# Splitting weights into two rounded parts: the low part made by a negating copy on ACT and an adding DMA, instead of a subtraction on DVE

## The chip, the cores and the metric

The kernel runs on one core of a Trainium2 chip. The metric is the device time of one execution in microseconds; a run reports the median of several. The profile is one execution taken by the hardware profiler. Its span runs from the first to the last instruction. The engines are TensorE (PE, with its weight loads as PEld), VectorE (DVE), ScalarE (ACT), GpSimd (POOL) and SyncE (SP). SP and POOL issue the DMAs here; each engine works through its own instructions in order.

## The reference

A decoder layer on 512 tokens of 1024 features, all in float32:

```
h = h + 1/2 * SwiGLU(RMSNorm(h))
u = RMSNorm(h); P = u @ W_in      # [b | c | v], [z | xBC | dt], [g_a | g_b]
y_a = W_out_a( b * conv3(c * v) )
y_b = W_out_ssm( GroupRMSNorm( SSD(conv4(xBC)) * silu(z) ) )
h = h + W_mix_out( sigmoid(g_a) * y_a + sigmoid(g_b) * y_b )
h = h + CrossAttn(RMSNorm(h), RMSNorm(mem))      # 4 heads, 256 memory tokens
h = h + 1/2 * SwiGLU(RMSNorm(h))
out = RMSNorm(h)
```

SSD is the chunked state-space product: chunks of 128 tokens, 32 heads in 4 groups, a state that is carried from chunk to chunk, and decays exp(acs[l] - acs[s]) inside a chunk. What matters here are the matrix products with weights, some 145 MB of them: each weight is read from DRAM once and used once.

## The kernel before

Activations lie feature-major, as tiles of 128 features by 512 tokens. Weights are the stationary operand of TensorE. TensorE multiplies in a rounded form of float32 (fp32r), so every product of 256 or more columns is made of three: hi*hi, hi*lo and lo*hi, where hi is an operand rounded to fp32r and lo is what the rounding took off.

Weights come in tiles of 128 partitions by up to 1024 columns (512 KB), which are 8 blocks of 128 by 128. `load_w` makes one such tile. It loads the raw tile `wr` by a DMA on SP's queue (L95), casts it to `wh` on ACT (L84), and subtracts `wl = wr - wh` on DVE (L85). Each of the three has three buffers. `job` then runs 24 products over the tile, three for each block: wh with the high part of the activations (L110), wh with their low part (L111), wl with their high part (L112). A job's result stands in one of five PSUM banks `pj`. The same `split` helper (L83 to L85) also splits activations, so L84 and L85 occur with other tiles too (sh and sl, ynh and ynl).

The stages, in order: a feed-forward part (44 column tiles of w_gu, then 8 of w_d, each of three weight tiles); the projections and the state-space part; the short convolution and the mixing (with h brought back from DRAM by nine DMAs on POOL's queue, L441 and L445); keys and values (w_k and w_v, with only 256 columns per product, or weights as the moving operand); queries, attention and its output; the second feed-forward part; and a final norm.

In the state-space part each group makes decay tiles `m`: SP loads a row of `acd` broadcast to all partitions (L360), POOL subtracts (L362), ACT takes two functions (L365, L366), DVE multiplies (L367), and TensorE uses them (L379). Between these, TensorE transposes x (L317), DVE makes xdt and xe from it (L320, L325), and a state product follows (L329). `btok` is a copy on ACT of transposed B (L309). The `w_os` jobs behind each group have half tiles of 256 KB.

The program's order on each engine is not that of the source. A scheduler interleaves the instructions when the program is built, by its own estimate of when each operand is ready, so work of the next group's projections stands between the steps of a group.

The first weight tile is loaded in two halves, ahead of everything else but one tile of h.

Of the kernel before, what the change touches and what calls it, by code (L numbers as in the profile page):

```python
"""Hybrid decoder layer (macaron SwiGLU, short-conv + SSD mixer, memory cross-attention, macaron
SwiGLU, final RMSNorm) on one core.

Activations lie feature-major ([128 features, 512 tokens] tiles), weights are the stationary operand.
Every float32 product of 256 or more moving columns is three float32r passes over operands split
exactly in two: hi*hi + hi*lo + lo*hi; narrower products are plain float32.
"""
# [1 line left out]

# [9 lines left out]
AF = mybir.ActivationFunctionType  # L19
ALU = mybir.AluOpType  # L20
# [3 lines left out]
T = 512  # L24
# [4 lines left out]
M = 256  # L29
NH = 32  # L30
NG = 4
MB = 4  # decay tiles in flight
PJ = 5  # PSUM banks of the projections; the other banks serve the rest
NC = 4
EPS = 1e-6

# [11 lines left out]
def layer(ctx: ExitStack, tc: tile.TileContext, a, out):  # L48
# [38 lines left out]
    def load_w(src, n, parts=1):  # L87
        if ahead:
            return ahead.pop(0)
        raw = wp.tile([P, 1024], F32, tag="wr", name=nm("wr"), bufs=3)  # L90
        hi = wp.tile([P, 1024], F32R, tag="wh", name=nm("wh"), bufs=3)
        lo = wp.tile([P, 1024], F32R, tag="wl", name=nm("wl"), bufs=3)
        for i in range(parts):
            c = slice(i * n // parts, (i + 1) * n // parts)
            nc.sync.dma_start(out=raw[:, c], in_=src[:, c])  # L95
            split(raw[:, c], hi[:, c], lo[:, c])
        return hi, lo

    def job(pt, w, xs, m=P):
        """pt += sum over k of w[k]^T xs[k]; w: DRAM [128, nk * m]; xs: (hi, lo) per k."""  # L100
        nk = len(xs)
        pieces = -(-nk // 8)
        per = -(-nk // pieces)
        for k0 in range(0, nk, per):
            k1 = min(nk, k0 + per)
            hi, lo = load_w(w[:, k0 * m:k1 * m], (k1 - k0) * m)
            for k in range(k0, k1):
                s_ = slice((k - k0) * m, (k - k0 + 1) * m)
                xh, xl = xs[k]
                TE.matmul(pt, hi[:, s_], xh, start=(k == 0), stop=False)  # L110
                TE.matmul(pt, hi[:, s_], xl, start=False, stop=False)  # L111
                TE.matmul(pt, lo[:, s_], xh, start=False, stop=(k == nk - 1))  # L112

    def gained(src, gname, k, pool, tag="u", bufs=8, n=T):
        """split src * gain into (hi, lo)"""
        hi = pool.tile([P, n], F32R, tag=tag + "h", name=nm("uh"), bufs=bufs)
        lo = pool.tile([P, n], F32R, tag=tag + "l", name=nm("ul"), bufs=bufs)
        g = pc(gname, k)
        S.activation(out=hi, in_=src, func=AF.Copy, scale=g)
        V.scalar_tensor_tensor(out=lo, in0=src, scalar=g, in1=hi, op0=ALU.mult, op1=ALU.subtract)  # L120
        return hi, lo

    def rms(tiles, n, pool, n_tok=T):
        """1 / sqrt(mean of squares + eps) over the features of tiles, for every token, on all
        partitions: [128, n_tok]"""
        nt = n_tok // P
        acc = None
        for k, t in enumerate(tiles):
            sq = pool.tile([P, T], F32, tag="sq", name=nm("sq"), bufs=3)[:, :n_tok]
            S.activation(out=sq, in_=t, func=AF.Square)  # L130
            if acc is None:
                acc = sq
            else:
                V.tensor_tensor(out=sq, in0=acc, in1=sq, op=ALU.add)  # L134
                acc = sq
        p1 = ps("ss")
        for c in range(nt):
            TE.matmul(p1[:, c:c + 1], acc[:, c * P:(c + 1) * P], ones[:, 0:1], start=True, stop=True)
        sd = pool.tile([P, 4], F32, tag="sd", name=nm("sd"), bufs=2)[:, :nt]
        S.activation(out=sd, in_=p1[:, :nt], func=AF.Sqrt, scale=1.0 / n, bias=eps)  # L140
        rc = pool.tile([P, 4], F32, tag="rc", name=nm("rc"), bufs=2)[:, :nt]
        V.reciprocal(out=rc, in_=sd)
        rb = pool.tile([P, T], F32, tag="sq", name=nm("rb"), bufs=3)[:, :n_tok]
        V.tensor_copy(out=rb.rearrange("p (c t) -> p c t", c=nt),
                      in_=rc.unsqueeze(2).to_broadcast([P, nt, P]))
        p2 = ps("ss")
        for c in range(nt):
            TE.transpose(p2[:, c * P:(c + 1) * P], rb[:, c * P:(c + 1) * P], ident)
        r = pool.tile([P, T], F32, tag="r", name=nm("r"), bufs=2)[:, :n_tok]
        S.copy(out=r, in_=p2[:, :n_tok])  # L150
        return r
# [44 lines left out]

    ffn("ffn1_norm", a["w_gu1"], a["w_d1"])

    # ---------------------------------------------------------------- mixer
    mo = ctx.enter_context(ExitStack())  # L200
    mop = mo.enter_context(tc.tile_pool(name="mo", bufs=1, reuse_waits="tile"))
    yb = [mop.tile([P, T], F32, tag=f"yb{k}", name=f"yb{k}") for k in range(KD)]
# [11 lines left out]
        return p  # L214

    def conv(wname, j0, ntap, acc, x):
        """acc[:, t] = sum over j of w[j] x[t - (ntap - 1) + j]; x in SBUF"""
        S.activation(out=acc, in_=x, func=AF.Copy, scale=pc(wname, j0 + ntap - 1))  # L218
        for j in range(ntap - 2, -1, -1):
            d = ntap - 1 - j  # L220
            V.scalar_tensor_tensor(out=acc[:, d:], in0=x[:, :T - d], scalar=pc(wname, j0 + j),  # L221
                                   in1=acc[:, d:], op0=ALU.mult, op1=ALU.add)

    with tc.tile_pool(name="mx", bufs=1, reuse_waits="tile") as mx:
# [1 line left out]
        def mt(tag, bufs, shape=(P, T), dt=F32):  # L226
            return mx.tile(list(shape), dt, tag=tag, name=nm(tag), bufs=bufs)

        # dt, decays
        pdt = ps()  # L230
        job(pdt[0:NH, :], a["w_dt"], u, m=NH)
        dtT = mt("cv", 2)
# [40 lines left out]
        acs3, dt3, dte3, eend3 = hc(acs), hc(dt), hc(dte), hc(eend)  # L273

        def xbc(ci, tag, bufs):
            """conv4 + silu of xBC feature tile ci"""
            p = proj(40 + ci)
            x = mt("cx", 2)
            V.tensor_tensor(out=x, in0=p, in1=r, op=ALU.mult)
# [12 lines left out]

        def ssd_state(g, bt, ct, xs):
            hs = slice(8 * g, 8 * g + 8)
            # C B^T, transposed, causal: [s, (c, l)]
            pcb = ps("ss")
            for c in range(NC):
                cs = slice(c * P, (c + 1) * P)
# [9 lines left out]
            btok = mt("btok", 1)  # L308
            S.copy(out=btok[:, :3 * P], in_=pbt[:, :3 * P])  # L309

            # token-major x * dt, x * dt * decay to the end of the chunk, states
            xdt, prev = [], []
            for c in range(NC):
                cs = slice(c * P, (c + 1) * P)
# [119 lines left out]
    with tc.tile_pool(name="mb", bufs=1, reuse_waits="tile") as mb:  # L434
# [9 lines left out]
        mem = xm.tile([P, KD, M], F32, tag="mem", name="mem")  # L444
        G.dma_start(out=mem, in_=a["memT"].rearrange("(k p) t -> p k t", p=P))  # L445

        # b * conv3(c * v)
        r2 = wt("r2", 1)
        S.activation(out=r2, in_=r, func=AF.Square)
        ya = []  # L450
# [35 lines left out]
            V.tensor_tensor(out=h[k], in0=p, in1=h[k], op=ALU.add)  # L486
    mo.close()

    # ---------------------------------------------------------------- cross attention
    with tc.tile_pool(name="xa", bufs=1, reuse_waits="tile") as xa:  # L490
        kT, vm = [], []
        with tc.tile_pool(name="xn", bufs=1, reuse_waits="tile") as xm:
# [123 lines left out]
                job(p, a["w_o"][k], o)  # L616
                V.tensor_tensor(out=h[k], in0=p, in1=h[k], op=ALU.add)

    # the final norm is applied token-major: 1 / rms is a scalar of the partition there
    ot = [None]  # L620
    acc = [None]

# [64 lines left out]


def _chunks(w, m=P):
    """(K, N) -> (N / m, 128, K / 128 * m): chunk c, row p holds w[k * 128 + p, c * m:(c + 1) * m]"""  # L690
    k, n = w.shape
    return np.ascontiguousarray(
        w.reshape(k // P, P, n // m, m).transpose(2, 1, 0, 3)).reshape(n // m, P, k // P * m)


def _rows(v):
    """(n * 128,) -> (128, n)"""
    return v.reshape(-1, P).T


def _taps(w):
    """(taps, n * 128) -> (128, n * taps)"""
    k, n = w.shape
    return w.reshape(k, n // P, P).transpose(2, 1, 0).reshape(P, -1)

# [42 lines left out]
```

## Time and profile before

| | us |
|---|---|
| median of 3 runs | 1629.68 (1629.1 to 1631.24) |
| span of the profiled execution | 1625.7 |
| TensorE busy | 1594.7 |
| DVE busy | 855.8 |
| ACT busy | 660.4 |
| POOL busy | 51.6 |

For the profiled execution itself only the span is given; the median of the timed runs lies 4.0 us above it. The granted clock of TensorE is 0.995 of full speed over the span.

A row of a group reads: line, engine, operation, output and inputs by their names in the program, shapes, count; then busy time and the mean of one; then the engine's idle time just before them and what ended most of it. A row of a DMA gives the size of one and the median time from its issue to its landing. A row of the timeline gives the start, the duration, and in brackets the idle time before and what ended it. A row of the waits gives who waited for whom, then the total, the times and the longest.

### The profile page before, as it was taken

The page shows a single profiled execution, that of the slowest core. Times are in us where ns is not written, and L with a number is a line of the kernel's source. Part 1 is how long each engine was busy: PE and PEld are TensorE (multiplying, and loading weights), DVE is VectorE, ACT ScalarE, POOL GpSimd, SP SyncE. Part 2 cuts the span into 40 slices and gives each one's busy share as a digit, 9 for nine tenths or more (in the row PEclk, how much of TensorE's full clock was granted, in tenths as well). Part 3 has the DMA queues.
Part 4 walks back from the last instruction along what each step waited for, and adds up shares of the span by engine and source line. Part 5 has one row for each costly group of instructions (what it writes and reads, how often), then busy time and mean ns, then how long its engine had stood idle before and what let it go on. Part 6 is the DMA issues. An engine that isn't in the chain of part 4 may idle for free.

```text
span 1625.7 us, 18647 instructions
## 1 busy us (share of the span) xinstructions
PE 1594.7 (98%) x7437; PEld 1303.2 (80%) x7437; DVE 855.8 (53%) x1134; ACT 660.4 (41%) x888; POOL 51.6 (3%) x54
## 2 busy tenths in 40 slices
PE   8999999999989999999999999999999999999997
PEld 6888888887768787787888888888878888888887
DVE  6343433346695786958564544565555434343332
ACT  6232322225768494765332223344443323232222
POOL 0000000000120110201010000000000000000000
PEclk9999999999999999999999999999999999999999
DMA  5323333333442333423253232235213232333331
GB/s 192 103 92 102 93 95 99 112 107 105 124 120 72 117 108 104 130 91 111 83 182 104 91 103 92 91 112 174 78 38 106 91 104 91 103 92 91 89 97 62
DMA packets 53911, 168.58 MB, mean 104 GB/s; under 512 B 6320, under 2 KB 6832, under 8 KB 53824
## 3 DMA queue, kind: packets, MB, share of 16 engines
q1 hardware_dynamic: 51952, 161.03, 32.1%
q0 software_dynamic: 1584, 5.31, 0.9%
q8 instruction: 58, 0.95, 0.2%
q10 hardware_dynamic: 288, 1.05, 0.2%
q14 instruction: 29, 0.24, 0.0%
HBM read 163.10 MB, written 4.26 MB: 103 GB/s over the span
## 4 chain that ended last, share of the span: by engine, by line
PE 57%; issue 1%; DVE 1%; ACT 0%; DMA 0%; DVEq 0%; ACTq 0%
PE pj L110 17%; PE pj L112 17%; PE pj L111 17%; PE pj L516 0%; PE pj L518 0%; PE pj L517 0%; PE ss L379 0%; PE pj L650 0%; PE pj L652 0%; PE pj L651 0%; DMA m<-acd 0%; PE ss L598 0%; PE ss L384 0%; PE ss L561 0%; PE ss L560 0%
## 5 line engine op out<-in xcount | busy, mean ns | idle before, releaser
L84 ACT CAST wh<-wr 128x1024 fp32r<-128x1024 f32 (+2 forms) x298 | 294.2, 988 | 805.5 <-PE pj L111 676.4
L110 PE MATMUL pj<-uh,wh 128*128 128x512 f32 x1416 | 555.7, 393 | 7.2 <-ACT wh L84 7.2
L112 PE MATMUL pj<-uh,wl 128*128 128x512 f32 x1416 | 554.4, 392 | 0.0
L111 PE MATMUL pj<-ul,wh 128*128 128x512 f32 x1416 | 553.7, 391 | 0.0
L85 DVE TENSOR_TENSOR wl<-wr,wh 128x1024 fp32r<-128x1024 f32 (+2 forms) x298 | 341.2, 1146 | 200.4 <-ACT wh L84 195.0
L110 PEld LDWEIGHTS pj<-uh,wh 128*128 128x128 f32 x1416 | 266.1, 188 | 63.3 <-ACT wh L84 7.2
L112 PEld LDWEIGHTS pj<-uh,wl 128*128 128x128 f32 x1416 | 266.3, 188 | 56.7 <-issue 0.7
L111 PEld LDWEIGHTS pj<-ul,wh 128*128 128x128 f32 x1416 | 266.3, 188 | 55.8 <-DVE ul L120 0.7
L110 PE MATMUL pj<-sh,wh 128*128 128x512 f32 x330 | 131.2, 398 | 0.0
L111 PE MATMUL pj<-sl,wh 128*128 128x512 f32 x330 | 130.8, 396 | 0.0
L112 PE MATMUL pj<-sh,wl 128*128 128x512 f32 x330 | 130.8, 396 | 0.0
L179 DVE TENSOR_TENSOR gt<-pj,gt 128x512 f32<-128x512 f32 x44 | 30.4, 692 | 137.2 <-PE pj L112 136.5
L177 DVE TENSOR_TENSOR gt<-pj,r 128x512 f32<-128x512 f32 x44 | 30.3, 692 | 112.9 <-PE pj L112 109.4
L112 PEld LDWEIGHTS pj<-sh,wl 128*128 128x128 f32 x330 | 62.2, 188 | 15.2
L110 PEld LDWEIGHTS pj<-sh,wh 128*128 128x128 f32 x330 | 62.2, 188 | 14.9
L111 PEld LDWEIGHTS pj<-sl,wh 128*128 128x128 f32 x330 | 62.2, 188 | 14.9
L221 DVE SCALAR_TENSOR_TENSOR cv<-cx,prm,cv 128x511 f32<-128x511 f32 (+2 forms) x72 | 63.3, 882 | 3.4 <-ACT cv L218 3.1
L362 POOL TENSOR_TENSOR m<-m,keep 128x512 f32<-128x512 f32 x32 | 41.2, 1301 | 313.0 <-DMA m<-acd 302.2
L111 PE MATMUL pj<-ynl,wh 128*128 128x512 f32 x128 | 50.7, 396 | 0.0
L112 PE MATMUL pj<-ynh,wl 128*128 128x512 f32 x128 | 50.7, 396 | 0.0
L110 PE MATMUL pj<-ynh,wh 128*128 128x512 f32 x128 | 50.7, 396 | 0.0
L134 DVE TENSOR_TENSOR sq<-sq,sq 128x512 f32<-128x512 f32 (+1 forms) x47 | 32.2, 685 | 2.5 <-ACT sq L130 1.7
(223 smaller groups left out, 1661.4 us busy)
## 6 DMA issues: line engine op xcount, KB each, us to landing
wr<-in_w_gu SPq DMA_DIRECT2D x87, 512.0 KB, 3.6
wr<-in_w_in SPq DMA_DIRECT2D x80, 512.0 KB, 3.6
wr<-in_w_d SPq DMA_DIRECT2D x32, 512.0 KB, 3.6
m<-acd SPq DMA_DIRECT2D x32, 256.0 KB, 3.8
wr<-in_w_os SPq DMA_DIRECT2D x32, 256.0 KB, 3.0
wr<-in_w_d SPq DMA_DIRECT2D x16, 384.0 KB, 3.1
ea<-acd SPq DMA_DIRECT2D x32, 128.0 KB, 4.5
wr<-in_w_oa SPq DMA_DIRECT2D x8, 512.0 KB, 3.5
```

The costliest lines, as they stand in the source:

```text
L84: S.copy(out=hi, in_=src)
L85: V.tensor_tensor(out=lo, in0=src, in1=hi, op=ALU.subtract)
L110: TE.matmul(pt, hi[:, s_], xh, start=(k == 0), stop=False)
L111: TE.matmul(pt, hi[:, s_], xl, start=False, stop=False)
L112: TE.matmul(pt, lo[:, s_], xh, start=False, stop=(k == nk - 1))
L134: V.tensor_tensor(out=sq, in0=acc, in1=sq, op=ALU.add)
L177: V.tensor_tensor(out=gt, in0=pg, in1=r, op=ALU.mult)
L179: V.tensor_tensor(out=gt, in0=pu, in1=gt, op=ALU.mult)
L221: V.scalar_tensor_tensor(out=acc[:, d:], in0=x[:, :T - d], scalar=pc(wname, j0 + j), in1=acc[:, d:], op0=ALU.mult, op1=ALU.add)
L362: G.tensor_tensor(out=m4, in0=m4, in1=acs[:, (h0 + hh) * NC:(h0 + hh + 1) * NC].unsqueeze(2) .to_broadcast([P, NC, P]), op=ALU.subtract)
```

## The change

In `load_w` the low part is made in another way. ACT writes the negated weight into `wl`, rounded as `wh` is because `wl` has the same type, and a DMA on POOL's queue reads the raw weight from DRAM a second time and adds it onto `wl`. The raw tile `wr` is then read by ACT alone. Activations are split as before, by `split`.

```diff
@@ load_w
         for i in range(parts):
             c = slice(i * n // parts, (i + 1) * n // parts)
             nc.sync.dma_start(out=raw[:, c], in_=src[:, c])
-            split(raw[:, c], hi[:, c], lo[:, c])
+            S.copy(out=hi[:, c], in_=raw[:, c])
+            S.activation(out=lo[:, c], in_=raw[:, c], func=AF.Copy, scale=-1.0)
+            G.dma_start(out=lo[:, c], in_=src[:, c], accum_op=ALU.add)
         return hi, lo
```

The rest of the diff takes out comments and docstrings without moving a line. The code behind `load_w` stands two lines lower: the cast of a weight is now L96, its negation L97, the adding DMA L98, and the three products of `job` are L112, L113 and L114.

The scheduler builds another order from this. On ACT, in the first feed-forward part, the program before had, with gt and sh the gate's activation and its high part:

```order
L178 ACTIVATE gt_518<-gt_518 128x512
L84 CAST wh_599<-wr_598 128x1024
L84 CAST sh_522<-gt_518 128x512
L84 CAST wh_629<-wr_628 128x1024
L178 ACTIVATE gt_588<-gt_588 128x512
```

and the changed one has, one column tile further on:

```order
L180 ACTIVATE gt_601<-gt_601 128x512
L96 CAST wh_684<-wr_683 128x1024
L97 ACTIVATE wl_685<-wr_683 128x1024
L84 CAST sh_605<-gt_601 128x512
L96 CAST wh_715<-wr_714 128x1024
L97 ACTIVATE wl_716<-wr_714 128x1024
```

The negation of a weight tile stands right behind its cast; the rest keeps its place.

On TensorE, in the state-space part of group 0, the program before had these products between the last of the first four transposes of x (L317) and the first state product (L329); pj_3215 is a job of the next group's projections:

```order
L317 MATMUL ss_2982<-con,xs_2831 128x128
L110 MATMUL pj_3215<-uh_2432,wh_3217 128x512
L111 MATMUL pj_3215<-ul_2433,wh_3217 128x512
L112 MATMUL pj_3215<-uh_2432,wl_3218 128x512
L110 MATMUL pj_3215<-uh_2436,wh_3217 128x512
L111 MATMUL pj_3215<-ul_2437,wh_3217 128x512
L112 MATMUL pj_3215<-uh_2436,wl_3218 128x512
L110 MATMUL pj_3215<-uh_2440,wh_3217 128x512
L111 MATMUL pj_3215<-ul_2441,wh_3217 128x512
L112 MATMUL pj_3215<-uh_2440,wl_3218 128x512
L110 MATMUL pj_3215<-uh_2444,wh_3217 128x512
L111 MATMUL pj_3215<-ul_2445,wh_3217 128x512
```

The changed one has there, with the transposes now L319 and the state product L331:

```order
L319 MATMUL ss_3062<-con,xs_2907 128x128
L112 MATMUL pj_3295<-uh_2501,wh_3297 128x512
L113 MATMUL pj_3295<-ul_2502,wh_3297 128x512
L331 MATMUL ss_3071<-xe_3069,btok_3060 128x512
L319 MATMUL ss_3075<-con,xs_2784 128x128
```

Eleven products of the job have become two, those that need the high part wh alone; its low part, wl_3298, is used only after two more rounds of transposes. In groups 1 to 3 ten products stand at this place, low part included. On ACT, at the same place, the negation that begins wl_3298 stands behind the copy btok, which waits for TensorE (L351 and z belong to the gate, L334 is a copy of a state):

```order
L96 CAST wh_3297<-wr_3296 128x1024
L351 ACT_TABLE_LOAD
L351 ACTIVATE z_3046<-z_3046 128x512
L311 COPY btok_3060<-ss_3056 128x384
L97 ACTIVATE wl_3298<-wr_3296 128x1024
L96 CAST wh_3338<-wr_3337 128x1024
L334 COPY prev_3073<-ss_3071 128x512
L97 ACTIVATE wl_3339<-wr_3337 128x1024
```

The cast and the negation of one tile, next to each other elsewhere, are three rows apart here.

On POOL, whose queue held only the decay subtractions in this part, weight DMAs now stand between them. At the change from group 0 to group 1 (m_3176 to m_3215 belong to group 0, m_3910 on to group 1):

```order
L364 TENSOR_TENSOR m_3215<-m_3215,keep 128x512
L364 TENSOR_TENSOR m_3910<-m_3910,keep 128x512
L364 TENSOR_TENSOR m_3916<-m_3916,keep 128x512
L98 DMA wl_3421<-in_w_in 128x1024
L364 TENSOR_TENSOR m_3943<-m_3943,keep 128x512
L98 DMA wl_3462<-in_w_in 128x1024
L364 TENSOR_TENSOR m_3949<-m_3949,keep 128x512
L98 DMA wl_3503<-in_w_in 128x1024
```

Each of these DMAs is issued only when the subtractions ahead of it, which wait for their own loads of m, are done.

## The prediction

> **What bounds the kernel now.** I read the busy table first, then the groups, then the waits.
>
> ```profile
> span 1625.7 us, 18647 instructions
> PE 1594.7 (98%) x7437; PEld 1303.2 (80%) x7437; DVE 855.8 (53%) x1134; ACT 660.4 (41%) x888; POOL 51.6 (3%) x54
> L84 ACT CAST wh<-wr 128x1024 fp32r<-128x1024 f32 x247 | 259.6, 1051 | 707.5 <-PE pj L111 586.1 <-issue 94.4 <-PE pj L112 11.7
> L85 DVE TENSOR_TENSOR wl<-wr,wh 128x1024 fp32r<-128x1024 f32 x247 | 302.2, 1224 | 178.6 <-ACT wh L84 173.1
> PE ss L379 <- DVE m L367: 9.0, 4, 2.6
> ```
>
> TensorE is busy for 98% of the span: 31 us of idle time are all that can be won. The casts wait for TensorE to free a buffer (586.1 us), not the other way round, so a weight tile is prepared ahead of need, and the 302 us of subtractions on DVE stand on no path. What TensorE does wait for on DVE is 9.0 us in the state-space part. So the change cannot win much; the question is whether its longer chain still fits under the matmuls.
>
> The cover is seen in the timeline of the first feed-forward part:
>
> ```profile
> 152.22 1.06 ACT L84 CAST wh<-wr 128x1024 fp32r<-128x1024 f32 x1 [3.84 <-PE pj L111]
> 153.19 0.62 ACT L84 CAST sh<-gt 128x512 fp32r<-128x512 f32 x1
> 157.66 1.05 ACT L84 CAST wh<-wr 128x1024 fp32r<-128x1024 f32 x1 [3.84 <-PE pj L111]
> ```
>
> A tile of 24 products lasts 157.66 - 152.22 = 5.44 us, 0.227 us a product. Three buffers: the cast at 152.22 starts as tile i-3 ends, and the tile's low part is first needed by its third product, two tiles and about two products later: 152.2 + 10.9 + 0.45 = 163.5 us. That is the due time.
>
> **The change, part by part.** It removes 298 subtractions on DVE (247 of full size, the rest smaller; worth nothing by the above, except in the state-space part). It adds 298 negations on ACT and 298 accumulating DMAs on POOL's queue. Nothing in the trace accumulates in a DMA, so I bound it by these rows:
>
> ```profile
> L178 ACT ACTIVATE gt<-gt 128x512 f32<-128x512 f32 x44 | 27.7, 632 | 0.5 <-DVE gt L177 0.5
> wr<-in_w_gu SPq DMA_DIRECT2D x87, 512.0 KB, 3.6
> wr<-in_w_os SPq DMA_DIRECT2D x32, 256.0 KB, 3.0
> hd<-h POOLq DMA_DIRECT2D x8, 256.0 KB, 3.1
> hb<-hd POOLq DMA_DIRECT2D x8, 256.0 KB, 5.4
> mem<-in_memT POOLq DMA_DIRECT2D x1, 1024.0 KB, 10.2
> 283.79 0.55 POOL L208 DMA_DIRECT2D hd<-h  x1 [14.81 <-DVE h L195]
> ```
>
> The negation: an ACTIVATE of 512 columns takes 632 ns, a cast of 512 takes 621 (the sh row above, 0.62), so for 1024 columns I take the cast's 1.05 us. The DMA: POOL's 256 KB land in 3.1 us against SP's 3.0, so its queue costs about 0.1 us more, with 0.55 us of POOL for one issue. 256 KB more cost SP 0.6 us (3.0 to 3.6). The add has to fetch the destination as well as the source; counting that as 512 KB more gives 3.6 + 1.2 = 4.8 us, and sharing the engines with the next raw tile (512 KB) another 1.2: **6.0 us**. Low end 3.6 (the destination costs nothing), high end 10.2 (the slowest row of this queue, which ran behind 2 MB of others).
>
> The Trainium skill, "Collectives: The Full Stack", section "The bandwidth ceiling: the fold count and why AG ≠ RS ≠ AR", says that the add inside a DMA costs no time, but that a reduce reads two sources through one ring and so runs at half the rate of a copy. By this rule the 1.2 us stand; were the add a single read, the term for keys and values below would be 0 and the sum 16. No run here shows it yet.
>
> Feed-forward and projection tiles: 152.22 + 0.97 (a cast to the next ACT start, 153.19) + 1.05 + 6.0 = 160.3, 3.2 us before it is due at 163.5. Term: **0**. With 10.2 us it would be 1.0 us late once in three tiles, 0.33 us × 247 = +82 us.
>
> The rate has to fit too. A tile now moves 0.52 MB; with the source read again and the destination read it moves 1.57 MB by my count.
>
> ```profile
> 20.00:268.00 248.00, 248.00 (x1099) 205.06 (x1098) 103.12 (x120) 76.28 (x95) 0.00 (x0) 1.00 0.32 97
> GB/s 107 50 135 313 356 392 328 371 264 399 385 392 399 427 420 378 406 385 349 342 349 356 406 370 257 135 264 370 143 7 0 0 0 0 0 0 0 0 121 221
> ```
>
> The first row (last two columns: DMA share and GB/s) says 97 GB/s now, so 3 × 97 = 291 after. The second, 817 to 840 us, shows POOL and SP together sustaining about 385. 291 fits, with a quarter to spare.
>
> **Keys and values** do not fit. Their tiles are as large and used in half the time:
>
> ```profile
> 1095.67 1.05 ACT L84 CAST wh<-wr 128x1024 fp32r<-128x1024 f32 x1 [1.50 <-PE pj L111]
> 1098.48 1.05 ACT L84 CAST wh<-wr 128x1024 fp32r<-128x1024 f32 x1 [1.50 <-PE pj L111]
> 1110.00:1120.00 10.00, 10.00 (x45) 8.04 (x44) 5.26 (x6) 5.10 (x6) 0.00 (x0) 1.00 0.62 184
> ```
>
> 2.81 us a tile, at 184 GB/s already. 1.57 MB at 385 GB/s are 4.09 us: 1.28 us more for each of 16 tiles, less two that lie ready: **+18 us**. Low end 0 (1.05 MB at 385 are 2.72 us); high end at 97 / 0.32 = 303 GB/s, 5.19 us, (5.19 - 2.81) × 14 = +33.
>
> **Start.** Nothing covers the first tile:
>
> ```profile
> 6.59 1.12 ACT L84 CAST wh<-wr 128x512 fp32r<-128x512 f32 x2
> 8.27 0.65 PE L112 MATMUL pj<-uh,wl 128*128 128x512 f32 x1
> h<-in_xT SPq DMA_DIRECT2D x8, 256.0 KB, 6.1
> ```
>
> The first half's cast ends at 7.15, its negation near 7.75. 256 KB land 3.6 us later (3.0 and the destination's 0.6) or, by the loads of h in flight at that time, 6.1: 11.4 to 13.9 instead of 8.27. The product of 8.27 is third in order and all others stand behind it: +3.1 to +5.6, I take **+4.3**.
>
> **State-space part**, four groups. The order shows two things. In group 0 the 11 products that ran between the first transposes and the state product are 2, and the negation stands behind the copy btok on ACT. On POOL, DMAs for weights now stand behind decay subtractions that wait for their own loads:
>
> ```profile
> 454.50 5.62 POOL L362 TENSOR_TENSOR m<-m,keep 128x512 f32<-128x512 f32 x4 [38.34 <-DMA m<-acd]
> L320 DVE TENSOR_TENSOR xdt<-ss,keep 128x512 f32<-128x512 f32 x16 | 10.9, 683 | 0.0
> L325 DVE TENSOR_TENSOR xe<-ss,keep 128x512 f32<-128x512 f32 x12 | 8.2, 681 | 0.0
> 440.00:500.00 60.00, 54.77 (x281) 42.45 (x280) 54.69 (x76) 37.86 (x51) 10.66 (x8) 0.94 0.34 101
> ```
>
> Group 0: the state product waits for xdt and xe, 1.36 us and some 0.3 of hand-over, with 2 products (0.45) as cover: 1.2 us, twice; and the low part of the first tile comes about 2 us late: +4.4. In groups 1 to 3 such products stay, and I charge 2 us each for weights held behind a subtraction (1.3 us each, four in 5.62): together **+10**. Low end -9 (all of L379's waits go, DVE being free: in 440 to 500 it is busy for 54.69 of 60 us). High end +22: the 5.62 us on the path in each group.
>
> **Reload of h.** The weight DMA for the third of the short-convolution tiles stands behind nine POOL DMAs.
>
> ```profile
> 817.36 4.28 POOL L441 DMA_DIRECT2D hb<-hd  x8 [60.30 <-PE pj L112]
> 821.98 0.90 POOL L445 DMA_DIRECT2D mem<-in_memT  x1 [0.34 <-issue]
> ```
>
> It can issue at 822.9 and lands 6.0 to 10.2 us later, at 828.9 to 833.1; TensorE needs it after two tiles and six products, 817.3 + 10.9 + 1.4 = 829.6: 0 to +3.5, I take **+2**. The half tiles of w_os: 256 KB, 0.52 + 0.62 + 4.2 = 5.3 us against two half tiles (5.44) and two products (0.45); 0, and +2 over 32 tiles with the 5.4 us of hb.
>
> **Sum:** 18 + 4.3 + 10 + 2 = 34.3 us; span 1625.7 + 34.3 = 1660.0. The median of the runs, 1629.68, is 4.0 above the span; I keep that: **1664 us**.
>
> **Rivals.** (1) The accumulating DMA bounds every stage. Raw data take 0.52 / 385 = 1.36 us of 5.44, leaving 4.08 for the add: below 128 GB/s of its own bytes TensorE waits everywhere. The mem row is 1024 KB in 10.2 us, 103 GB/s, so this is near. At 115 GB/s a tile takes 4.56 + 1.36 = 5.92: 0.48 × 247 = +119, keys and values (5.92 - 2.81) × 16 = +50, the rest 16: 1815 us. Against it: that row had 2 MB ahead of it. (2) All is hidden but the start, +3.1, and DVE gives that back in the state-space part: 1630. For it: the add's own engine time is unseen. (3) Faster: if the destination's read costs nothing, keys and values lose nothing (2.72 under 2.81 us: the point from which it decides), the start costs 3.1, and DVE, without its 1.22 us subtractions, takes back all 9.0 us of L379's waits: 1624. Against it: m on DVE comes from ACT's exponentials, and ACT gets 1.05 us more per tile.
>
> **How the numbers follow.** Forecast 0.58, rival (1) 0.28, (2) 0.08, (3) 0.06. 0.2% is 3.3 us, about what a measurement can tell. Faster 0.06, same 0.08, slower 0.86. The range leaves out (2), (3) and the quarter of (1) that lies above 1850: 1634 to 1850. It holds all bounds of the forecast's own terms but the 10.2 us DMA at its worst.
>
> **What would show it.** In the profile after: the DMA rows wl near 6 us to landing in feed-forward stages, and no wait of L114 on them there; tiles at 4.1 us between 1085 and 1135 with L114 waiting on the DMA; the first low product near 12.5 us; waits at L331 in group 0. A landing time above 9 us, or a DMA share near 1 in the feed-forward stages, would make me wrong by rival (1).

## The result, and the profile after

The changed kernel takes **1755.26 us** (median of 4 runs, 1747.09 to 1755.87) against 1629.95 us (4 runs): **1.0759 times** the time before, 95% interval 1.0738 to 1.0781. The profiled execution has a span of 1753.0 us at a granted clock of 0.974, where the kernel before had 1625.7 us at 0.995. So the loss that has to be explained is 127.3 us of span; 34.3 were forecast.

The page's busy table and its queues (packets, megabytes, share of 16 engines' span):

```profile
span 1753.0 us, 19399 instructions
PE 1634.4 (93%) x7437; PEld 1320.6 (75%) x7437; DVE 527.5 (30%) x836; ACT 900.6 (51%) x1173; POOL 303.7 (17%) x352
q0 software_dynamic: 44496, 150.16, 47.3%
q1 hardware_dynamic: 51952, 161.03, 32.0%
```

DVE gave away 328 us and ACT took 240 us more, and neither is near its span. TensorE has the same 7437 products, but is idle for 1753.0 - 1634.4 = 118.6 us in place of 31.0, and its busy time grew by 39.7 us: 87.6 and 39.7 make the 127.3. The software queue (POOL's, with the accumulating DMAs) moves fewer bytes than the hardware queue (SP's) and occupies the engines half as long again.

The page's DMA issues (KB of one, median time to landing), and the group of POOL's issues; the last row is the loads of m in the kernel before:

```profile
wr<-in_w_gu SPq DMA_DIRECT2D x87, 512.0 KB, 5.5
wl<-in_w_gu POOLq DMA_DIRECT2D x87, 512.0 KB, 7.7
wl<-in_w_in POOLq DMA_DIRECT2D x80, 512.0 KB, 7.7
m<-acd SPq DMA_DIRECT2D x32, 256.0 KB, 6.3
L98 POOL DMA_DIRECT2D wl<-in_w_gu x89 | 76.7, 862 | 409.7 <-ACT wl L97 404.4
```

```profile
m<-acd SPq DMA_DIRECT2D x32, 256.0 KB, 3.8
```

An addition lands after 7.7 us, where I took 6.0, and costs POOL 0.86 us to issue, where a plain one cost 0.55. The other loads land later too: a raw tile of w_gu after 5.5 us instead of 3.6, a row for m after 6.3 instead of 3.8.

What TensorE waits for (total, times, longest):

```profile
PE pj L114 <- DMA wl<-in_w_in: 39.4, 14, 8.0
PE ss L381 <- DVE m L369: 17.4, 4, 5.6
PE pj L114 <- DMA wl<-in_w_k: 10.4, 4, 5.0
PE pj L114 <- DMA wl<-in_w_os: 9.4, 10, 3.5
PE pj L519 <- DMA wl<-in_w_v: 8.8, 4, 3.5
PE pj L114 <- DMA wl<-in_w_gu: 7.6, 3, 7.2
PE ss L331 <- DVE xe L327: 2.7, 2, 1.7
```

L114 is the product with the low part `wl`, and L519 the one of w_v. None of these weight waits exists in the kernel before. Of those on w_in and w_os, 30.0 and 9.4 us lie in the projections and the state-space part, where only 10 us were forecast.

To place the loss I cut both traces at the same seven products: the first that uses sh, the last of ynh with wl, the first of yah, the last of mgh, the last of w_v, the last of oh, the last of sh with wl (the ends of the groups by tile). The table gives the length of each stretch, less that of before.

| us added in the profiled execution | forecast | after |
|---|---|---|
| start and first feed-forward part | 4.3 | 8.2 |
| projections and state-space part | 10 | **71.0** |
| reload of h, short convolution | 2 | 12.5 |
| mixing | 0 | 0.0 |
| keys and values | 18 | 28.7 |
| attention | 0 | 4.8 |
| second feed-forward part, end | 0 | 2.1 |
| together | 34.3 | 127.3 |

Kernels below that share the code of a stage differ there by up to some 3 us from one profile to another, so a difference of that size in this table or the next means nothing.

**Where the chain fits.** The timeline of the first feed-forward part, ACT's rows and POOL's:

```profile
154.83 1.05 ACT L96 CAST wh<-wr 128x1024 fp32r<-128x1024 f32 x1 [2.92 <-issue]
155.79 1.05 ACT L97 ACTIVATE wl<-wr 128x1024 fp32r<-128x1024 f32 x1
157.13 0.86 POOL L98 DMA_DIRECT2D wl<-in_w_gu  x1 [4.58 <-ACT wl L97]
160.27 1.06 ACT L96 CAST wh<-wr 128x1024 fp32r<-128x1024 f32 x1 [2.91 <-issue]
```

A tile still takes 160.27 - 154.83 = 5.44 us. By the median, the addition lands at about 157.13 + 7.7 = 164.8, and by the prediction's rule it is due at 154.83 + 10.9 + 0.45 = 166.2. It is in time, with 1.4 us to spare, not 3.2. Over the stretch 60 to 260 us (row of the windows: stretch, busy time of PE, PEld, DVE, ACT and POOL, clock, DMA share, GB/s) TensorE never stops:

```profile
60.00:260.00 200.00, 200.00 (x884) 165.42 (x883) 38.06 (x55) 92.55 (x111) 31.36 (x37) 1.00 0.91 194
```

**Where it doesn't.** The same chain in group 0 of the state-space part:

```profile
453.10 1.03 ACT L96 CAST wh<-wr 128x1024 fp32r<-128x1024 f32 x1
456.73 1.06 ACT L97 ACTIVATE wl<-wr 128x1024 fp32r<-128x1024 f32 x1
458.08 0.86 POOL L98 DMA_DIRECT2D wl<-in_w_in  x1 [15.53 <-ACT wl L97]
458.64 1.10 PE L331 MATMUL ss<-xe,btok 128*128 128x512 f32 x2 [1.67 <-DVE xe L327]
461.64 1.10 PE L331 MATMUL ss<-xe,btok 128*128 128x512 f32 x2 [1.00 <-DVE xe L327]
466.19 0.79 PE L114 MATMUL pj<-uh,wl 128*128 128x512 f32 x1 [3.01 <-DMA wl<-in_w_in]
```

The negation follows its cast after 3.6 us instead of 1.0 (the table load, z and btok shown in the order stand between). That alone is more than the 1.4 us to spare, and TensorE waits 3.01 us for the landing 8.1 us after the issue. The two waits at L331 are those the prediction named, 1.67 and 1.00 us for the 1.2 and 1.2 it charged.

**Where the 71.0 us are.** Within the stretch of the projections and the state-space part, TensorE waits 39.4 us for the low part, 8.4 us more than before for m (17.4 against 9.0), and its busy time is 22.5 us longer. The waits for m belong to the decay chain, whose loads land later, as shown above; that this makes them longer was not tried apart. Neither they nor the longer busy time had a term in the forecast.

**What a wait leaves behind.** TensorE's timeline goes on like this after the wait at 466.19; the windows below it give its busy time and, third from the end of a row, the granted clock:

```profile
466.78 0.63 PE L112 MATMUL pj<-uh,wh 128*128 128x512 f32 x1
467.21 0.63 PE L113 MATMUL pj<-ul,wh 128*128 128x512 f32 x1
```

```profile
462.59:466.00 3.41, 0.59 (x5) 0.35 (x3) 2.48 (x4) 0.62 (x1) 0.86 (x1) 1.00 0.95 238
466.00:469.41 3.41, 3.22 (x8) 2.55 (x9) 0.00 (x0) 0.00 (x0) 0.00 (x0) 0.50 1.05 264
469.41:472.82 3.41, 3.41 (x29) 2.21 (x27) 1.29 (x2) 0.00 (x0) 0.00 (x0) 1.00 0.83 192
```

Products start 0.43 us apart behind the wait, where a product of the feed-forward part takes 0.227 us. The clock is at half rate from 466.00 to 469.41. This is most of the 39.7 us of busy time. Over all stretches at half rate TensorE is busy for 67.2 us in the changed kernel and for 10.4 us in the one before; half of the difference, 28 us, is my estimate of what the clock took, and the other 11 us are not explained here. The Trainium skill, "TensorE: Matmul & The Clock Gate", section "Part 1: The HAM clock gate (the "warmup" mystery)", says that TensorE's clock is halved after an idle window of about 3.4 us and comes back after about as long of steady work; the trace agrees on the half rate and on the length of 3.41 us, but a wait of 3.01 us was enough here, and shorter ones were elsewhere (last section).

### The profile page after: what moved, and what is told of

Read it like the earlier page. It is cut to its first block, busy times and chain, and to the rows that moved or that the text cites. A ratio compares the mean times of both kernels' runs of the same rounds, so it can differ in the third digit from the quotient of the medians.

```text
span 1753.0 us, 19399 instructions
## 1 busy us (share of the span) xinstructions
PE 1634.4 (93%) x7437; PEld 1320.6 (75%) x7437; DVE 527.5 (30%) x836; ACT 900.6 (51%) x1173; POOL 303.7 (17%) x352
## 3 DMA queue, kind: packets, MB, share of 16 engines
q0 software_dynamic: 44496, 150.16, 47.3%
## 4 chain that ended last, share of the span: by engine, by line
PE 55%; issue 26%; DMA 12%; POOL 4%; ACT 2%; DVE 1%; POOLq 0%; SPq 0%; DVEq 0%; ACTq 0%
PE pj L114 17%; PE pj L112 17%; PE pj L113 17%; DMA wl<-in_w_in 4%; POOL wl L98 3%; DMA m<-acd 2%; DMA wl<-in_w_v 1%; DMA wl<-in_w_os 1%; DMA wl<-in_w_gu 1%; DMA wl<-in_w_k 1%; PE ss L381 1%; DMA wl<-in_w_d 1%; PE ss L331 1%; PE ss L386 0%; DMA wl<-in_w_o 0%
## 5 line engine op out<-in xcount | busy, mean ns | idle before, releaser
L96 ACT CAST wh<-wr 128x1024 fp32r<-128x1024 f32 (+2 forms) x298 | 294.1, 987 | 690.2 <-issue 599.6
L114 PE MATMUL pj<-uh,wl 128*128 128x512 f32 x1416 | 560.3, 397 | 46.9 <-DMA wl<-in_w_in 39.4
L112 PE MATMUL pj<-uh,wh 128*128 128x512 f32 x1416 | 559.4, 395 | 7.4 <-ACT wh L96 7.3
L113 PE MATMUL pj<-ul,wh 128*128 128x512 f32 x1416 | 559.1, 395 | 0.0
L114 PEld LDWEIGHTS pj<-uh,wl 128*128 128x128 f32 x1416 | 269.0, 190 | 109.6 <-DMA wl<-in_w_in 44.7
L112 PEld LDWEIGHTS pj<-uh,wh 128*128 128x128 f32 x1416 | 269.6, 190 | 64.0 <-ACT wh L96 7.8
L113 PEld LDWEIGHTS pj<-ul,wh 128*128 128x128 f32 x1416 | 268.6, 190 | 57.5 <-issue 1.0
L97 ACT ACTIVATE wl<-wr 128x1024 fp32r<-128x1024 f32 (+2 forms) x298 | 295.3, 991 | 11.3 <-PE pj L519 11.3
L98 POOL DMA_DIRECT2D wl<-in_w_gu x89 | 76.7, 862 | 409.7 <-ACT wl L97 404.4
L98 POOL DMA_DIRECT2D wl<-in_w_in x80 | 69.0, 869 | 377.4 <-ACT wl L97 360.5
L112 PE MATMUL pj<-sh,wh 128*128 128x512 f32 x330 | 131.2, 398 | 0.0
L114 PE MATMUL pj<-sh,wl 128*128 128x512 f32 x330 | 131.0, 397 | 0.1
L113 PE MATMUL pj<-sl,wh 128*128 128x512 f32 x330 | 130.8, 396 | 0.0
L98 POOL DMA_DIRECT2D wl<-in_w_d x48 | 41.4, 863 | 206.3 <-ACT wl L97 206.3
L114 PEld LDWEIGHTS pj<-sh,wl 128*128 128x128 f32 x330 | 62.1, 188 | 16.0 <-DMA wl<-in_w_d 1.0
L113 PEld LDWEIGHTS pj<-sl,wh 128*128 128x128 f32 x330 | 62.1, 188 | 14.9
L112 PEld LDWEIGHTS pj<-sh,wh 128*128 128x128 f32 x330 | 62.2, 188 | 14.7
L195 DVE SCALAR_TENSOR_TENSOR dn<-pj,r 128x512 f32<-128x512 f32 x15 | 10.4, 692 | 184.7 <-PE pj L114 184.7
L223 DVE SCALAR_TENSOR_TENSOR cv<-cx,prm,cv 128x509 f32<-128x509 f32 (+2 forms) x72 | 56.3, 796 | 22.1 <-ACT cv L220 21.3
L114 PE MATMUL pj<-ynh,wl 128*128 128x512 f32 x128 | 53.1, 416 | 9.6 <-DMA wl<-in_w_os 9.4
```

The source lines that it names most:

```text
L96: S.copy(out=hi[:, c], in_=raw[:, c])
L97: S.activation(out=lo[:, c], in_=raw[:, c], func=AF.Copy, scale=-1.0)
L98: G.dma_start(out=lo[:, c], in_=src[:, c], accum_op=ALU.add)
L195: V.scalar_tensor_tensor(out=dn, in0=pd, scalar=0.5, in1=r, op0=ALU.mult, op1=ALU.mult)
```

## The experiments

Theory: the chain of a tile's low part has become longer than the lead that three buffers give, by the read of the destination above all, and wherever ACT's or POOL's queue delays it TensorE waits. Rivals: ACT's added 240 us; POOL's queue, in which weights stand behind decay subtractions; the accumulating DMA's rate, which no lead could mend; a disturbance in one stage that shifts all later ones. Each kernel below is the changed one with the edit shown, and e11 is the kernel before with half tiles. An edit can also make the scheduler build another order: by their traces, e2 alone has the changed kernel's order of TensorE, ACT and POOL in every place. The time of the kernel before on the same chip was 1627.7 to 1628.4 us. This is the stage table of their profiled executions, in us against the kernel before:

| | start, FFN 1 | state-space | reload | mixing | keys, values | attention | FFN 2, end |
|---|---|---|---|---|---|---|---|
| changed kernel | 8.2 | 71.0 | 12.5 | 0.0 | 28.7 | 4.8 | 2.1 |
| e1 DVE adds | 1.7 | 5.8 | 0.0 | 0.0 | -0.9 | 0.0 | -0.1 |
| e2 plain copy | 8.2 | 28.4 | 8.6 | 0.0 | 6.6 | 0.0 | 0.3 |
| e3 decay on DVE | 9.6 | 54.8 | 10.4 | 0.1 | 25.8 | 7.0 | 2.1 |
| e4 subtraction in state-space | 8.7 | 0.0 | 10.7 | 0.0 | 27.5 | 7.7 | 1.9 |
| e5 copy, decay on DVE | 7.8 | 8.8 | 8.2 | 0.0 | 7.0 | 0.3 | -0.2 |
| e6 four low tiles | 8.2 | 37.5 | 12.1 | 0.0 | 23.8 | 2.7 | -0.2 |
| e7 half added | 7.0 | 19.9 | 3.1 | 0.0 | 10.1 | 0.4 | -0.5 |
| e8 only feed-forward | 4.5 | -1.9 | 0.0 | 0.0 | 0.0 | 0.0 | 1.1 |
| e9 half tiles | 7.3 | 19.5 | 6.4 | 0.0 | 16.8 | 0.1 | -0.6 |
| e10 half tiles, decay on DVE | 7.1 | 7.4 | 5.1 | 0.0 | 16.7 | 0.1 | -0.5 |
| e11 half tiles, subtracted | 0.4 | 0.7 | 0.1 | 0.0 | -0.9 | -0.4 | -0.5 |
| e12 reload on SP | 10.9 | 70.8 | 6.6 | 0.2 | 25.5 | 7.4 | 2.0 |

### ACT's part: the addition on DVE

```diff
-            G.dma_start(out=lo[:, c], in_=src[:, c], accum_op=ALU.add)
+            V.tensor_tensor(out=lo[:, c], in0=raw[:, c], in1=lo[:, c], op=ALU.add)
```

> ACT still writes the negated weight, but DVE adds the raw weight instead of a DMA. If the 125 us come from the DMA's path (its latency, POOL's queue, or the DMA engines), they go: 1630 us, at most 1640. If ACT's 298 more instructions of 1.05 us are what hurts in the state-space part, most of its 71 us stay: 1680 to 1700.

1634.51 us, ratio 1.0048 (1.0025 to 1.007): the first case. ACT does all the negations of the changed kernel, and 5.8 of the 71 us in the state-space part are left. The rest of the loss hangs on the DMA.

### The read of the destination: a plain copy

```diff
-            G.dma_start(out=lo[:, c], in_=src[:, c], accum_op=ALU.add)
+            G.dma_start(out=lo[:, c], in_=src[:, c])
```

> The DMA overwrites the low part with the raw weight and adds nothing, so the destination is not read; everything else stands as in the changed kernel (the low part is wrong by that, only the time counts). If the read of the destination is what costs, the landing falls from 7.7 us to about 5, keys and values lose under 10 us instead of 28.7, and the state-space part loses half of its 71: about 1695. If waiting in POOL's queue is what costs in the state-space part, its 71 us hardly move: 1730 or more.

1676.16 us, ratio 1.0298 (1.0248 to 1.0349), better than expected. What each DMA waits for, the number of DMAs and the source bytes are the same; only the addition is gone. Rows of its page (issues, queue, POOL's group), to be set beside those of the changed kernel above:

```profile
wl<-in_w_gu POOLq DMA_DIRECT2D x87, 512.0 KB, 4.6
wl<-in_w_in POOLq DMA_DIRECT2D x80, 512.0 KB, 4.8
q0 software_dynamic: 44496, 150.16, 25.6%
L98 POOL DMA_DIRECT2D wl<-in_w_gu x89 | 47.2, 530 | 438.5 <-ACT wl L97 438.5
```

Its windows, for the same 200 us of the feed-forward part:

```profile
60.00:260.00 200.00, 200.00 (x884) 165.57 (x883) 38.02 (x55) 92.52 (x111) 19.19 (x37) 1.00 0.59 194
```

The addition costs 3 us of landing, 0.33 us of POOL a tile, and a DMA share of 0.91 for 0.59 in the same stretch. One packet of this queue takes 0.473 × 1753.0 × 16 / 44496 = 0.298 us with it and 0.256 × 1677.8 × 16 / 44496 = 0.154 us without: 1.93 times. The rule that the prediction weighed, from the Trainium skill, "Collectives: The Full Stack", section "The bandwidth ceiling: the fold count and why AG ≠ RS ≠ AR" (a reduce runs at half the rate of a copy), agrees with this. By the stage table the addition is worth 42.6 us in the state-space part and 22.1 in keys and values, but nothing at the start: there the copy loses 8.2 us just the same.

### Whether stages disturb each other: subtraction in the state-space part

```diff
+            if not dma_add[0]:
+                split(raw[:, c], hi[:, c], lo[:, c])
+                continue
...
     ffn("ffn1_norm", a["w_gu1"], a["w_d1"])
+    dma_add[0] = False
```

(with True again behind the state-space part)

> The projections and the state-space part make the low part by the old subtraction on DVE, all other stages by the DMA. If the stages lose each for itself, 71 us go and the rest stays: 1684. If losses only move (a stall there hides one elsewhere), the time is above 1700.

1685.72 us, ratio 1.0357 (1.0327 to 1.0387), as expected. The state-space part loses 0.0 and every other stage what it lost before, within 3 us. Stages lose each for itself.

### POOL's queue: the decay's subtraction on DVE

```diff
-                    G.tensor_tensor(out=m4, in0=m4,
+                    V.tensor_tensor(out=m4, in0=m4,
```

> The decay subtractions of the state-space part are moved from POOL to DVE, so that POOL's queue holds weight DMAs and nothing that waits for the loads of m. If weight DMAs held behind those subtractions make the loss of 71 us, 40 us or more of it go: 1715 or less. If the length of the DMA's path alone makes it, the time stays within 15 us of 1755.

1732.85 us, ratio 1.0647 (1.0582 to 1.0712): between the two expectations. 16.2 us of the state-space part go, 54.8 stay. The same edit on top of the plain copy:

> The addition is left out (the DMA overwrites the negated tile with the raw weight, so the output is off by that) and the decay's subtraction moves from POOL to DVE. If the longer transfer and POOL's queue are two separate losses, each takes away its own: 1676 us of the plain copy less the 20 us that the moved subtraction brought, about 1656, with +10 left in the state-space part in place of +28. If POOL's queue only hurts because the transfer behind it is long, the plain copy has already removed it: 1670 to 1680, the state-space part still at +25 to +28.

1659.74 us, ratio 1.0189 (1.0172 to 1.0206): the first case by its numbers, two separate losses. It takes 28.4 - 8.8 = 19.6 us from the state-space part. But these are not weights held in POOL's queue. TensorE's waits in this part are, first in the plain copy (e2), then with the subtraction moved as well (e5):

```profile
PE ss L381 <- DVE m L369: 13.1, 6, 4.1
PE pj L114 <- DMA wl<-in_w_in: 7.8, 5, 3.2
PE pj L114 <- DMA wl<-in_w_os: 2.0, 1, 2.0
```

```profile
PE ss L381 <- DVE m L369: 7.5, 4, 2.5
PE pj L114 <- DMA wl<-in_w_in: 8.9, 5, 3.4
PE pj L114 <- DMA wl<-in_w_os: 2.7, 2, 2.2
```

The waits for the low part do not fall (9.8 and 11.6 us). The waits for m fall by 5.6 us, 4.6 us of waits for xe and for a norm go, and the busy time falls by 11.3 us, at a clock of 0.99 instead of 0.97 over the part. On the changed kernel (e3) the same move takes 3.6 us from the waits for the low part, 5.4 from those for m, and 4.7 from those for xe and the norm. So what the move gives back is mostly waits for m, xe and the norm, and the slow clock behind waits. A part of that is order and not POOL: in group 0 ten products stand ahead of the first state product in e3 and e5, where the changed kernel and e2 have two, and with the ten no wait for xe is left. No run keeps the order and moves the subtraction. A weight held behind a subtraction is seen once at length: the DMA issued at 421.66 in the changed kernel, 6 us after its negation, for which TensorE waits 5.17 us; in e3 three shorter waits stand there, 5.9 us together. The kernel before waits 9.0 us for m as well, and it was not run with the subtraction on DVE either, so a part of the 19.6 may have nothing to do with the change.

Taken off in this order, the 71.0 us are 42.6 for the addition, 19.6 for moving the decay's subtraction, order included, and 8.8 that are left, little more than the 5.8 of e1, which has no weight DMA on POOL at all.

### Half the bytes added

```diff
-            S.activation(out=lo[:, c], in_=raw[:, c], func=AF.Copy, scale=-1.0)
-            G.dma_start(out=lo[:, c], in_=src[:, c], accum_op=ALU.add)
+            S.activation(out=lo[:, f], in_=raw[:, f], func=AF.Copy, scale=-1.0)
+            G.dma_start(out=lo[:, f], in_=src[:, f], accum_op=ALU.add)
+            V.tensor_tensor(out=lo[:, g_], in0=raw[:, g_], in1=hi[:, g_], op=ALU.subtract)
```

(f and g_ are the first and the second half of the columns of c)

> Of each tile's low part the DMA adds one half of the columns, and DVE subtracts the other half as before the change; the number of DMA issues, their place in POOL's queue and ACT's place in the order stay, the bytes and the negated columns are half. If the transfer's length is the cause, it lands in about 5 us instead of 7.7 and the time comes near the plain copy's: 1670 to 1695 us. If the number of issues and the order set it, 1740 or more.

1666.82 us, ratio 1.0237 (1.0217 to 1.0256): by the transfer's length, and a little more than expected. There are as many DMAs, in the same queue, but those of w_gu and w_in land in 5.3 and 5.4 us, and the state-space part loses 19.9 us. ACT's negation is half as long too, so the transfer is not the only link that got shorter. The start still loses 7.0, though its first addition is now 128 KB.

### One more tile of lead

```diff
-        raw = wp.tile([P, 1024], F32, tag="wr", name=nm("wr"), bufs=3)
+        raw = wp.tile([P, 1024], F32, tag="wr", name=nm("wr"), bufs=2)
-        lo = wp.tile([P, 1024], F32R, tag="wl", name=nm("wl"), bufs=3)
+        lo = wp.tile([P, 1024], F32R, tag="wl", name=nm("wl"), bufs=4)
-            S.copy(out=hi[:, c], in_=raw[:, c])
             S.activation(out=lo[:, c], in_=raw[:, c], func=AF.Copy, scale=-1.0)
             G.dma_start(out=lo[:, c], in_=src[:, c], accum_op=ALU.add)
+            S.copy(out=hi[:, c], in_=raw[:, c])
```

> Four buffers of the low part instead of three and two of the raw weight instead of three, with the negation ahead of the cast, so that an addition may start one tile earlier. If the loss is latency (a tile's chain is longer than the lead that three buffers give), one tile of lead, 4 to 6 us, covers most waits: 1680 to 1710 us, keys and values back from +28 to under +12. If the loss is throughput (the accumulating queue can't move more bytes in these stages), or the lead is set by the order of ACT's stream and not by buffers, the time stays within 15 us of 1755.

1708.79 us, ratio 1.0498 (1.0473 to 1.0522). The total lies within the first case, but keys and values went to 23.8 and not below 12. In the state-space part half of the loss went, as latency says. The run is not clean: the negation also moved ahead of the cast, and with two raw buffers the raw loads come late in their turn, and the chain that ended last now has them in it, with 3% of the span on w_in's. It could not tell why keys and values stayed; the next three could.

### Latency or rate: tiles of half the size

```diff
-        raw = wp.tile([P, 1024], F32, tag="wr", name=nm("wr"), bufs=3)
-        hi = wp.tile([P, 1024], F32R, tag="wh", name=nm("wh"), bufs=3)
-        lo = wp.tile([P, 1024], F32R, tag="wl", name=nm("wl"), bufs=3)
+        raw = wp.tile([P, 512], F32, tag="wr", name=nm("wr"), bufs=6)
+        hi = wp.tile([P, 512], F32R, tag="wh", name=nm("wh"), bufs=6)
+        lo = wp.tile([P, 512], F32R, tag="wl", name=nm("wl"), bufs=6)
...
-        pieces = -(-nk // 8)
+        pieces = -(-nk // 4)
```

(and w_v, the first tiles and the last tile's loads in half pieces likewise)

> Weights come in tiles of 512 columns instead of 1024, six buffers of each kind instead of three: the same bytes, the same buffer memory, twice as many DMAs. A half tile's chain (negation 0.6, issue 0.9, landing about 5 us) is 6.5 us against a lead of five half tiles, 13.6 us, where a whole tile has 9.6 against 10.9. If the state-space part loses by latency and keys and values lose by the engines' rate, the first falls from +71 to +25 to +40 (POOL's queue stays) and the second stays at +24 to +32: 1690 to 1720 us in all. If rate is the cause in both, or POOL's issue time is, nothing falls: 1745 or more. If latency is the cause in both, keys and values fall below +12.

> As the half tiles, and the decay's subtraction on DVE instead of POOL. With latency and POOL's queue as the two causes in the state-space part, that part comes to within +5 to +15 of the kernel before; keys and values stay at +24 to +32: 1675 to 1695 us. If a third cause is at work there (ACT's longer stream, DMA traffic), +30 or more stays.

> The control of the two others: the kernel before, subtraction on DVE, with half tiles. Within 8 us of the kernel before, 1622 to 1638; what it loses or gains is to be taken off the two others.

1668.64 us, ratio 1.0243 (1.022 to 1.0266); 1661.91 us, ratio 1.0213 (1.0186 to 1.0241); and the control 1628.02 us, ratio 1.0006 (0.9995 to 1.0016). With the same bytes, the same buffer memory and twice the additions, the state-space part loses 19.5 us instead of 71.0, and 7.4 with the subtraction on DVE. The control gains nothing, so it is the chain that got shorter: latency, then what the moved subtraction gives. (The profiled execution of e9 was the longest of its four, 8.5 us above their median.) Both totals are lower than expected, because keys and values fell as well, to 16.8 and 16.7 us: neither the "stays" of rate alone nor the "below 12" of latency alone. They stop at a rate, which e9 shows in TensorE's timeline (three rows of a longer run of such waits), and in the windows below it:

```profile
1147.89 0.50 PE L519 MATMUL pj<-wl,mnh 128*128 128x512 f32 x1 [0.26 <-DMA wl<-in_w_v]
1149.94 0.49 PE L519 MATMUL pj<-wl,mnh 128*128 128x512 f32 x1 [0.38 <-DMA wl<-in_w_v]
1151.89 0.50 PE L519 MATMUL pj<-wl,mnh 128*128 128x512 f32 x1 [0.28 <-DMA wl<-in_w_v]
```

```profile
1120.00:1150.00 30.00, 23.92 (x170) 20.73 (x168) 4.84 (x10) 20.83 (x41) 13.77 (x16) 1.00 1.06 249
```

A half tile every 4.00 / 2 = 2.0 us, each waiting for its addition, at a DMA share of 1.06: 4.0 us for a whole tile, where 4.09 were forecast from 385 GB/s. POOL is busy for 13.77 of the 30 us and ACT for 20.83, so neither is full. In the changed kernel this stage took 47.2 + 28.7 = 75.9 us for 16 tiles, 4.74 each, with the DMA share at 0.91 and the clock at 0.87:

```profile
1173.00:1250.00 77.00, 56.35 (x292) 47.77 (x291) 9.89 (x22) 39.36 (x54) 13.76 (x16) 0.87 0.91 219
```

So, taking e9's loss for the rate's part, of 28.7 us some 17 are rate and some 12 are latency on top, with the half clock behind its waits.

### The reload's place in the queue

```diff
-            G.dma_start(out=h[k], in_=hd[k])
+            nc.sync.dma_start(out=h[k], in_=hd[k])
...
-        G.dma_start(out=mem, in_=a["memT"].rearrange("(k p) t -> p k t", p=P))
+        nc.sync.dma_start(out=mem, in_=a["memT"].rearrange("(k p) t -> p k t", p=P))
```

> The nine loads of the reload (h and mem) go through SP's queue instead of POOL's; all else as changed. If the reload loses because weight DMAs stand behind them in POOL's queue, as the prediction put it, its +12.5 falls to +4 or less and the time to 1743 to 1749 us. If it loses because 3 MB more are to be moved while each tile already moves three times its bytes, it stays at +8 to +13, and the raw weights behind these loads on SP's queue may even come later: 1750 to 1760.

1750.76 us, ratio 1.0754 (1.0737 to 1.0772), which tells nothing from 1755.26. In its own stage the loss fell from 12.5 to 6.6 us, halfway between the cases. The longest wait there was the one at 918.75 in the changed kernel, for the DMA issued at 905.27 behind the nine; the longest left is the one at 902.17 in this kernel:

```profile
905.27 0.90 POOL L98 DMA_DIRECT2D wl<-in_w_in  x1 [0.40 <-issue]
918.75 0.80 PE L114 MATMUL pj<-uh,wl 128*128 128x512 f32 x1 [7.99 <-DMA wl<-in_w_in]
```

```profile
902.17 0.50 PE L114 MATMUL pj<-uh,wl 128*128 128x512 f32 x1 [2.68 <-DMA wl<-in_w_in]
```

The negation of that tile ended at 898.35, so POOL's queue held its DMA for some 6.6 us (a free one follows its negation by 0.29), and it landed some 13.4 us after its issue. On SP's queue the reload takes both away. What makes the 6.6 us that are left was not taken apart. Three kernels with this stage as in the changed one (itself, e3, e4) lose 10.4 to 12.5 us in it, so 6.6 is a difference, but the share is rough.

### Where nothing should be lost: the feed-forward parts alone

```diff
+            if not dma_add[0]:
+                split(raw[:, c], hi[:, c], lo[:, c])
+                continue
...
+    dma_add[0] = True
     ffn("ffn1_norm", a["w_gu1"], a["w_d1"])
+    dma_add[0] = False
```

(and the last feed-forward part likewise; the two tiles loaded ahead of everything are subtracted)

> The DMA adds in the two feed-forward parts alone (behind the first two tiles); elsewhere DVE subtracts as before the change. If the long transfer is hidden wherever tiles are three deep ahead and PE is never short, the time is the kernel before's within 4 us: 1626 to 1632. If the traffic of these stages (a DMA share of 0.9) or ACT's 1 us a tile costs there and was only masked by the losses elsewhere, 1638 or more.

1636.4 us, ratio 1.0057 (1.004 to 1.0075): between the two cases. The stage table puts 4.5 us at the start, and there TensorE's timeline has a wait for the third tile; the windows have none at the end of the part:

```profile
25.75 0.50 PE L118 MATMUL pj<-uh,wl 128*128 128x512 f32 x1 [2.51 <-DMA wl<-in_w_gu]
```

```profile
200.00:255.00 55.00, 55.00 (x244) 45.56 (x243) 10.47 (x16) 25.57 (x31) 8.60 (x10) 1.00 0.88 193
```

The start's loss has moved to the first tile that is added, and behind it TensorE waits for a weight of this part once more, for 0.39 us. The profiled execution was the fastest of the four timed ones (1631.2 us); what the others lose beyond its 4 us was not traced. No version here beats the kernel before.

## Why the prediction was right in direction and wrong in size

- **What bounds the kernel.** Right: DVE's 302 us of subtractions were off the path; without them no stage got shorter.
- **Feed-forward tiles at 0.** Right as a result (200.00 of 200 us busy), by less than I thought: the landing is 7.7 us and not 6.0, and 1.4 us are left of the 3.2. Rival (1), that the addition bounds every stage, is refuted: behind the start the feed-forward tiles lose nothing, and mixing loses nothing. Its sign, a DMA share near 1, was there all the same (0.91), so the sign was badly chosen.
- **The state-space part at +10, with +22 as high end. This is the step that failed**: 71.0 us. I read off the order that weights stand behind subtractions and that a negation is late, and charged each such place once: "In groups 1 to 3 such products stay, and I charge 2 us each for weights held behind a subtraction". What I didn't do is make the due-time sum again for the tiles of this part: the term of 0 for "Feed-forward and projection tiles" was read from the feed-forward part alone. With 1.4 us to spare, a delay of a cast, a negation or an issue makes a tile late, and TensorE waits 39.4 us for the low part here. 42.6 us of the loss go with the addition (e2). The charge for weights held behind subtractions (6 in all) was put on the wrong wait: 19.6 us go when the subtraction leaves POOL (e5 against e2), but mostly from waits for m, xe and the norm and from the clock, and partly by another order of products. 8.8 are left. All but 7.4 go when the chain is short against its lead and the subtraction is off POOL (e10).
- **The clock.** No term had it. Each wait of 3 us or more was followed by some 3 to 5 us of slow products, and so were most of 2 us or more; 39.7 of the 127.3 us are busy time, an estimated 28 of them by the clock. A wait of TensorE costs more than its length.
- **Keys and values at +18.** The mechanism and the rate were right: at 4.09 us a tile forecast, the stage runs at 4.0 once its chain is short, and loses 16.8 (e9). The other 12 us were latency, which I left out where rate already decided. That the destination's read moves as bytes, as I counted, no run shows by itself; e9 bears out the product of count and rate.
- **Start at +4.3, at most +5.6.** Named rightly, sized wrongly: 7.5 us for the first low product (15.78 instead of 8.27). The page's DMA issues give 8.4 us to landing as the median of the two halves, not 6.1; the timeline has POOL's issue and the product, which starts 7.7 us after it:

```profile
wl<-in_w_gu POOLq DMA_DIRECT2D x2, 256.0 KB, 8.4
```

```profile
8.12 1.90 POOL L98 DMA_DIRECT2D wl<-in_w_gu  x2 [7.67 <-ACT wl L97]
15.78 0.80 PE L114 MATMUL pj<-uh,wl 128*128 128x512 f32 x1 [7.23 <-DMA wl<-in_w_gu]
```

  The addition isn't the reason, since a plain copy loses as much (e2) and 128 KB nearly so (e7); the only thing that the three share is a POOL transfer behind the loads of h and of the next tiles. That it is their traffic was not tried.
- **Reload at +2, at most +3.5.** 12.5: the place in POOL's queue was right, but the landing, taken as 6.0 to 10.2 us, was 13.4. With the reload on SP's queue half of the loss goes (e12); the cause of the other half is open.
- **Attention at 0.** 4.8: one wait of 2.3 us for w_o, with a stretch of half clock behind it.
- **The bounds.** +22 for the state-space part was one POOL wait per group on the path; it was no bound, since it held the landing at 6.0. The 10.2 us that I had as high end for the landing was applied to the quiet chain of the feed-forward part alone, counted for all 247 tiles.

## What to carry to other kernels

When a step in a prefetch chain gets longer, make the sum "start, each link, landing, due time" in every stage and with the queues of that stage, not once where the stage is quiet: 1.4 us to spare held where the queues were quiet, and gave 39.4 us of waits for the low part where they were not. Halving the tiles at the same buffer memory shortens each link and lengthens the lead, and it also tells latency (which goes) from rate (which stays). A stall of TensorE of 2 us or more should be priced with the slow clock that may follow it.

## What the runs showed that was not expected

- A DMA share of 0.91 is not 91% of what the engines can do. In the feed-forward part the changed kernel moved 194 GB/s at that share; in keys and values e9 moved 249 GB/s, over a stretch of 30 us, at 1.06. The share counts the time packets are under way, and packets that add take 1.93 times as long.
- The clock came down after waits of about 2 us too, as in these rows (a wait, and the windows around its end):

```profile
1229.60 0.50 PE L519 MATMUL pj<-wl,mnh 128*128 128x512 f32 x1 [2.04 <-DMA wl<-in_w_v]
```

```profile
1227.17:1230.58 3.41, 1.37 (x6) 0.84 (x5) 0.00 (x0) 1.95 (x2) 0.86 (x1) 1.00 1.08 278
1230.58:1233.99 3.41, 3.41 (x9) 2.65 (x9) 0.69 (x1) 1.11 (x2) 0.00 (x0) 0.50 1.02 270
```

  The half-rate stretches of the changed kernel, the last one aside, last 3.41 us or a multiple of it, and in the 3.41 us ahead of each TensorE was busy for at most 1.6 us. A wait of 2.08 us that ended at 805.07 brought none: it fell partly before and partly after 803.92, and TensorE was busy for 2.47 of the 3.41 us on one side and 2.26 on the other. The kernel before has the same in small: two of its three waits of 2.6 us for m were followed by 3.41 us at half rate.
